# A decoder layer on one core: a PSUM bank of their own for the attention projection's half steps, early merge loads, another form of the last norm

## The chip, the cores and the metric

One core of one Trainium2 chip runs the whole kernel. TensorE (PE) multiplies, VectorE (DVE), ScalarE (ACT) and GpSimd (POOL) do the rest, and SyncE (SP) issues most transfers. The metric is the device time of one execution in microseconds (us).

## The reference, cut to what matters

One step of a hybrid decoder layer for 512 prompt tokens and 8 x 4 sample tokens (544 in all), `D` = 1024, everything in float32:

```
x <- LN1(alpha*x + 1/2 * gate1 * SwiGLU_1(mod1(x)))
x <- LN2(alpha*x + gate2 * MIX(mod2(x)))
x <- LN3(alpha*x + 1/2 * gate3 * SwiGLU_2(mod3(x)))
y_a = rwkv7_time_mix(...)          # 8 heads x 64, delta-rule state
y_b = nsa attention(...)
m = (g_a * (y_a @ w_out_a) + g_b * (y_b @ w_out_b)) @ w_o
layer_norm: ((x - mean) * rsqrt(var + 1e-5)) * g + b
```

The change touches how `y_b @ w_out_b` is fitted in among the recurrence that gives `y_a`, how the sum of the two gated projections (the merge) gets its operands, and LN3, which gives the output `y`.

## The kernel before

Activations lie with features on the 128 partitions and tokens along the free axis, in 8 feature tiles of 128 x 544 (`xT`). A float32 product is made of three fast ones: every operand is split into a high part (`whi`, an ACT cast, L261) and a low part (`wlo`, a DVE subtraction, L179), and TensorE multiplies high by high, high by low and low by high. A product of one 128-column weight tile over 544 tokens is done as two halves of 272 tokens.

The stages follow each other: first FFN, input projections, attention, the RWKV recurrence, the merge of both branches, the output projection `w_o` with LN2, the second FFN, and LN3 (`LayerNormOut`). A scheduler places the instructions of a stage by priorities when the program is built; on the chip each engine runs its own list strictly in order, and semaphores hold an instruction until its data and its buffers are there.

**Recurrence (about 1020 to 1250 us).** `rw_head` makes one of four pairs of heads; up to four are alive, a new one starting some steps after the last. A head has a front (decays, products of 64 x 64 and 128 x 128), a forward substitution that runs on DVE (tiles `t` and `x`), then many narrow products (32 x 32 by L1687, L1695, L1713; 32 x 512 by L1817), prompt steps one after another (L1780 to L1802) and a tail that writes the head's features to `yah` (high and low part). Nearly all its small results go through `sm()`, the pool `smp` of four PSUM banks; wide ones through `mm()`, two pairs of banks.

**The attention projection `wob_steps`** runs inside this stage, at a lower priority than the heads, one half step at a time when a head says that it has only small work: 12 matmuls of 128 x 128 x 272 into one `sm()` bank (L288 on tiles `ybh`), then a DVE operation that multiplies by the gate (`gst`). After two half steps the tile is stored to device memory (`mbd`, by SP, L1978). There are 8 x 2 half steps.

**Merge (L2026 to L2065).** For each of 8 feature tiles: the weight `w_out_a` (256 KB), the gate `gdr` and `mbd` (272 KB each) are loaded by SP, three tiles ahead; 24 matmuls (L2040) make the product from `yah`; DVE multiplies by the gate, adds `mbd` and makes the low part `ul`; ACT makes the high part `uh`. The old `xT` (272 KB) is loaded back as well. For the first two tiles the three quarters of the product that don't need the last head (k = 0..2) are issued ahead. All loads and weight buffers of this stage come from pools that open only when those of the recurrence are closed. Then eight loads of `w_o` (512 KB) follow on the same queue.

**Second FFN start.** Casts of its weights (L261) share ACT with LN2's normalisation of 8 feature tiles (`xT<-xT,pv`, L193). f counts the column blocks of the gate and up weights; f = 0 and 1 are loaded early.

**LN3.** `feature(qt, k)` transposes feature tile k of 128 tokens into PSUM (L710), `bn_stats` (L712) on DVE every four tiles, and `finish(qt)` does statistics, square root, reciprocal, and then for both halves of 512 features: ACT scales and shifts, DVE multiplies by `ln_g`, POOL or DVE adds `ln_b` (L731), SP stores (L732). Tokens 0 to 255 are handled while the last product still runs on the others; tokens 256 to 511 and the sample tokens come at the end.

## Time and profile before

| | us |
|---|---|
| three runs: lowest, median, highest | 1766.15, 1773.29, 1776.47 |
| profiled execution: device time | 1771.6 |
| profiled execution: span | 1769.4 |
| PE busy in the span | 1666.9 (94%) |
| DVE, ACT, POOL busy | 879.5, 603.1, 242.3 |
| mean granted TensorE clock | 0.974 of full |

In a view by windows a row gives a stretch, its length, the busy us of PE, PE's weight loads, DVE, ACT and POOL with instruction counts, then the granted TensorE clock (1.00 is 2.4 GHz, 0.50 is 1.2 GHz), the share of the DMA engines and the GB/s. In a timeline a row is start, length, engine, line, operation, out<-in, shapes, count, and in brackets the idle time ahead with its releaser. The chain that ended last names, back from the end, what each piece of work had waited for. SPq is the queue of SP. Matmul ends are modelled, so lengths of matmuls overlap; the distance of starts is the cost of one.

### The profile page before, as it was taken

The numbers are of one execution on the slowest core, as the hardware profiler recorded it, in microseconds if no ns is written. First come the engines' busy times: TensorE is split into PE (matmuls) and PEld (weight loads), VectorE is DVE, ScalarE is ACT, GpSimd is POOL, SyncE is SP. The second block draws the span as 40 slices with busy tenths as digits, with TensorE's granted clock in tenths as the row PEclk, the third lists the DMA queues.
The fourth block names the chain that finished last, engine by engine and source line by source line (L and its number), as shares of the span: only waits on it lengthen the run. The fifth ranks groups of instructions, "written<-read, shape, count | busy, mean of one in ns | idle before, by whom it ended". The sixth has DMA issues, their size and how long they took to land.

```text
span 1769.4 us, 34773 instructions
## 1 busy us (share of the span) xinstructions
PE 1666.9 (94%) x14710; PEld 1515.0 (86%) x14710; DVE 879.5 (50%) x1834; ACT 603.1 (34%) x1095; POOL 242.3 (14%) x290
## 2 busy tenths in 40 slices
PE   5999999999999899898998999999799999999995
PEld 4888899999999888677786978777788999999994
DVE  6664233223335736555567277675677233233345
ACT  4343221221224543334445333332456221222221
POOL 6640000000000213545300021111011000000001
PEclk9999999999999999999999989997899999999998
DMA  7863662653434285565431431201742232323321
GB/s 275 303 192 114 196 195 87 194 193 113 143 105 99 89 262 160 171 203 159 122 110 49 123 100 32 65 22 34 241 115 89 86 89 85 94 76 96 91 63 51
DMA packets 261788, 224.98 MB, mean 127 GB/s; under 512 B 28880, under 2 KB 225915, under 8 KB 261376
## 3 DMA queue, kind: packets, MB, share of 16 engines
q1 hardware_dynamic: 246008, 182.60, 34.6%
q0 software_dynamic: 9728, 33.56, 5.9%
q10 hardware_dynamic: 5896, 6.60, 1.1%
q8 instruction: 116, 1.90, 0.5%
q14 instruction: 40, 0.33, 0.1%
HBM read 199.55 MB, written 23.17 MB: 126 GB/s over the span
## 4 chain that ended last, share of the span: by engine, by line
PE 79%; DVE 7%; issue 5%; DMA 3%; ACT 3%; POOL 2%; SPq 0%; ACTq 0%; POOLq 0%; DVEq 0%
PE mm L279 45%; PE mm L288 7%; PE mm L400 5%; PE sm L519 2%; PE sm L288 2%; PE sm L1817 1%; PE mm L2040 1%; PE mm L1519 1%; POOL sraw L1217 1%; PE sm L1163 1%; PE sm L1655 1%; DMA raw<-in_phi_w1t_dram 1%; PE sm L1627 1%; PE mm L1125 1%; DVE xT L173 1%
## 5 line engine op out<-in xcount | busy, mean ns | idle before, releaser
L261 ACT CAST whi<-raw 128x1024 fp32r<-128x1024 f32 (+2 forms) x178 | 177.5, 998 | 657.9 <-PE mm L279 591.8
L279 PE MATMUL mm<-uh,whi 128*128 128x272 f32 (+1 forms) x1888 | 397.2, 292 | 2.5 <-ACT qs L193 1.3
L279 PE MATMUL mm<-uh,wlo 128*128 128x272 f32 (+1 forms) x1888 | 392.5, 289 | 0.3 <-DVE wlo L179 0.3
L279 PE MATMUL mm<-ul,whi 128*128 128x272 f32 (+1 forms) x1888 | 391.9, 288 | 0.0
L179 DVE TENSOR_TENSOR wlo<-raw,whi 128x1024 fp32r<-128x1024 f32 (+2 forms) x178 | 207.0, 1163 | 267.8 <-ACT whi L261 266.3
L279 PEld LDWEIGHTS mm<-uh,whi 128*128 128x128 f32 x1888 | 298.0, 189 | 21.8 <-ACT hh L797 9.2
L279 PEld LDWEIGHTS mm<-ul,whi 128*128 128x128 f32 x1888 | 299.8, 189 | 1.0 <-issue 1.0
L279 PEld LDWEIGHTS mm<-uh,wlo 128*128 128x128 f32 x1888 | 297.3, 189 | 1.7 <-DVE sg L173 0.8
L173 DVE TENSOR_TENSOR sg<-mm,sg 128x544 f32<-128x544 f32 (+1 forms) x47 | 32.3, 688 | 164.4 <-PE mm L279 159.4
L676 POOL TENSOR_TENSOR xT<-xT,mr 128x272 f32<-128x272 f32 x24 | 25.0, 1059 | 600.6 <-DVE xT L173 591.1
L400 PE MATMUL mm<-cx,w1h 128*128 128x256 f32 x512 | 99.8, 290 | 3.7 <-ACT cx L352 1.9
L279 PE MATMUL mm<-hh,whi 128*128 128x256 f32 x480 | 99.3, 288 | 0.0
L279 PE MATMUL mm<-hh,wlo 128*128 128x256 f32 x480 | 99.0, 288 | 0.0
L279 PE MATMUL mm<-hlo,whi 128*128 128x256 f32 x480 | 98.9, 287 | 0.0
L400 PEld LDWEIGHTS mm<-cx,w1h 128*128 128x128 f32 x512 | 82.0, 192 | 11.2 <-issue 6.7
L279 PEld LDWEIGHTS mm<-hh,whi 128*128 128x128 f32 x480 | 76.7, 188 | 1.7 <-ACT hh L797 1.7
L279 PEld LDWEIGHTS mm<-hlo,whi 128*128 128x128 f32 x480 | 76.9, 188 | 0.0
L279 PEld LDWEIGHTS mm<-hh,wlo 128*128 128x128 f32 x480 | 76.8, 188 | 0.0
L400 PE MATMUL mm<-cx,w1l 128*128 128x256 f32 x256 | 73.5, 287 | 0.0
L1217 POOL DMA_INDIRECT sraw<-in_cache_kv_sel_dram,idx x64 | 63.9, 998 | 58.1 <-DMA t_new_kv_win_sample_dram<-sraw 22.6
L182 DVE SCALAR_TENSOR_TENSOR xT<-mm,modT,xT 128x512 f32<-128x512 f32 (+2 forms) x80 | 46.3, 581 | 37.0 <-PE mm L288 37.0
L738 DVE TENSOR_TENSOR rtmp<-mm,modT 128x32 f32<-128x32 f32 x32 | 6.1, 192 | 117.0 <-PE mm L279 117.0
(529 smaller groups left out, 2959.9 us busy)
## 6 DMA issues: line engine op xcount, KB each, us to landing
araw<-in_w_ada_dram SPq DMA_DIRECT2D x56, 512.0 KB
raw<-in_ffn_w_gate_dram SPq DMA_DIRECT2D x44, 512.0 KB
raw<-in_ffn_w_up_dram SPq DMA_DIRECT2D x44, 512.0 KB
raw<-in_w_in_dram SPq DMA_DIRECT2D x36, 512.0 KB
raw<-in_ffn_w_down_dram SPq DMA_DIRECT2D x32, 448.0 KB
raw<-in_w_ada_dram SPq DMA_DIRECT2D x16, 512.0 KB
raw<-in_ffn_w_down_dram SPq DMA_DIRECT2D x16, 512.0 KB
sraw<-in_state_kv_win_dram SPq DMA_DIRECT2D x16, 256.0 KB
```

The source lines that it names most:

```text
L173: V.tensor_tensor(out, a, b, ALU.mult)
L179: V.tensor_tensor(out, a, b, ALU.subtract)
L182: V.scalar_tensor_tensor(out, a, s, b, o0, o1)
L261: S.copy(hv, raw)
L279: T.matmul(ps[:m, h, :n], ww[:, k, :m], xx[:, c0:c0 + n], start=(k == 0 and j == 0), stop=(k == nk - 1 and j == 2))
L288: T.matmul(ps[:, :n], ww[:, k, :], xx[:, c0:c0 + n], start=(k == 0 and j == 0), stop=(k == nk - 1 and j == 2))
L400: T.matmul(pss[:, o, 256 * v:256 * v + 256], ww[:, v, o, jj, :], xx, start=(jj == 0 and j == 0), stop=(jj == 7 and j == 2))
L519: T.matmul(hold["ps"][32 * q:32 * q + 32, :], silT[:, k, :], raws_[i][:, h * 512:(h + 1) * 512], start=(k == 0), stop=(k == KT - 1), tile_ ...
L676: G.tensor_tensor(n, n, mr, ALU.subtract)
L1125: T.matmul(ps[:, g, 0:nk], qT[64 * g:64 * g + 64, i, qt * 128:(qt + 1) * 128], kvt[br, 0][64 * g:64 * g + 64, 0:nk], start=True, stop=True)
L1163: T.matmul(acc[64 * g:64 * g + 64, kt * 128:], kvtok[br][:, kt, 128 + 64 * g:192 + 64 * g], pt_[g][:, 512 * kt:384 * kt + 512], start=(br ...
L1217: G.indirect_dma_start(out=t, out_offset=None, in_=seltab, in_offset=bass.IndirectOffsetOnAxis(ap=idx8[:, c * NB + b:c * NB + b + 1], axis=0))
```

## The change

1. PSUM: `smp` (four banks) is closed when the heads are created. The heads' small products then use three banks (`smr`), and the half steps of `wob_steps` one bank of their own (`wb`). After the merge's first parts there are four again (`sm2`).
2. `mbd` is stored by POOL's queue instead of SP's.
3. Merge: the weights of tiles 0 and 1 are loaded and split from the recurrence's own pool, and the parts k = 0..2, then k = 3, are issued before that pool closes. Gates and `mbd` go into the rows of the result tiles `u[0]`, `u[1]` that they end in, four tiles ahead. The load of `xT` tile n is held until tile n is merged, by a POOL copy of one column from `ga`.
4. LN3 of tokens 256 to 543: `late(k)` transposes g·x (scaled by ACT), and keeps running sums of x and x squared; `close()` adds these up over the partitions by matmuls with ones, and corrects the transposed tiles in PSUM by one matmul per bank with rows of -g and b, so that a single scaled copy is left for each bank. The rows are prepared at LN3's construction, near the second FFN's start (memset, four row loads, a cast, a subtraction, two row copies by DMA, two ACT operations on 64 x 1024).

```diff
+    stm = ExitStack()
+    smp = pool("smp", 4, PSUM, stack=stm)
...
             for h in range(2):
                 cs = slice(HT * h, HT * h + HT)
-                ps = sm()
+                ps = wbp.tile([128, 512], F32, tag="wb", name=nm("wb"))
                 dense_half([ps], [w], lambda k: (ybh[0][:, k, :], ybh[1][:, k, :]), 4, HT * h, HT)
...
-            SY.dma_start(mbd[n], g_)
+            G.dma_start(mbd[n], g_)
...
     heads = [rw_head(ht) for ht in range(4)]
+    stm.close()
+    smp = pool("smr", 3, PSUM, stack=stm)
+    wbp = pool("wbp", 1, PSUM, stack=stm)
...
+    def merge_w(n):
+        return load_w(wview(woa, 0, 512, n * 128, (n + 1) * 128))
...
+    parts = [(mm(), merge_w(n)) for n in range(2)]
+    for p in parts:
+        merge_part(*p, 0, 3)
+    for p in parts:
+        merge_part(*p, 3, 4)
     str_.close()
     strp.close()
+    stm.close()
+    smp = pool("sm2", 4, PSUM, stack=stm)
...
     def merge_load(n):
-        raw = load_raw(wview(woa, 0, 512, n * 128, (n + 1) * 128))
-        t = [op.tile([128, TOK], F32, tag=tag, name=f"{tag}{n}", bufs=6) for tag in ("gate", "mb")]
-        SY.dma_start(t[0], gdr[0, n])
-        SY.dma_start(t[1], mbd[n])
-        return raw, t
+        if n < KT:
+            if n > 1:
+                raws[n] = load_raw(wview(woa, 0, 512, n * 128, (n + 1) * 128))
+            SY.dma_start(u[0][:, n, :].bitcast(F32), gdr[0, n])
+            SY.dma_start(u[1][:, n, :].bitcast(F32), mbd[n])
...
-        stt(v272(ga), v272(ga), 1.0, halves(ps), ALU.add, ALU.mult)
-        add(ga, ga, mb)
+        ga = op.tile([128, TOK], F32, tag="ga", name=nm("ga"), bufs=3)
+        stt(v272(ga), v272(u[0][:, n, :].bitcast(F32)), 1.0, halves(ps), ALU.add, ALU.mult)
+        add(ga, ga, u[1][:, n, :].bitcast(F32))
         S.copy(u[0][:, n, :], ga)
         sub(u[1][:, n, :], ga, u[0][:, n, :].bitcast(F32))
+        G.tensor_copy(xT[:, n, 0:1], ga[:, 0:1])
         SY.dma_start(xT[:, n, :], xsp[:, n, :])
...
+        def late(self, k):
+            z = xT[:, k, 256:TOK]
...
+            act(sq, z, AF.Square)
+            act(self.xs[:, k, :], z[:, 256:], AF.Copy, scale=gcol)
+            act(self.xg[k % 3], z[:, 0:256], AF.Copy, scale=gcol)
...
+                for o_, a, b in zip(self.run, self.old, (z, sq)):
+                    add(o_, a, b)
...
+            for j in range(2):
+                T.matmul(self.ps[j][k // 4][:, (k % 4) * 128:(k % 4 + 1) * 128],
+                         self.xg[k % 3][:, 128 * j:128 * j + 128], ident, is_transpose=True, start=(k % 4 == 0), stop=False)
+        def close(self):
...
+            st = mm()
+            for j, tag in enumerate("zq"):
+                hi, lo = [lnp.tile([128, NL], F32R, tag=tag + c_, name=nm("lh")) for c_ in "hl"]
+                S.copy(hi, self.run[j])
+                sub(lo, self.run[j], hi.bitcast(F32))
+                T.matmul(st[:, j, 0:NL], onesr, hi, start=True, stop=False)
+                T.matmul(st[:, j, 0:NL], onesr, lo, start=False, stop=False)
+                T.matmul(st[:, j, 0:NL], onesr.bitcast(F32), self.last[j], start=False, stop=True)
+            A, B, sg, lhs = slice(0, 64), slice(64, 128), self.sg, self.lhs
+            act(sg[B], st[B, 0, 0:NL], AF.Square)
+            S.copy(lhs[A], st[A, 0, 0:NL])
+            sub(sg[B], st[B, 1, 0:NL], sg[B])
+            sub(lhs[32:64], st[32:64, 0, 0:NL], lhs[32:64].bitcast(F32))
+            act(sg[B], sg[B], AF.Sqrt, bias=eps_ln[B])
+            V.tensor_copy(lhs[B], sg[B])
+            sub(lhs[96:128], sg[96:128], lhs[96:128].bitcast(F32))
...
+            for q, dst, m, ps in out:
+                yo = self.wk.tile([128, D], F32, tag="yo", name=nm("yo"), bufs=3)
+                for hf in range(2):
+                    c = slice(512 * hf, 512 * hf + 512)
+                    T.matmul(ps[hf][:m], lhs[:, 128 * q:128 * q + m], self.rows[:, c], start=False, stop=True)
+                    if hf == 0:
+                        act(yo[:m, c], ps[hf][:m], AF.Copy, scale=r[:m, q:q + 1])
+                    else:
+                        ts(yo[:m, c], ps[hf][:m], r[:m, q:q + 1], None, ALU.mult, ALU.bypass)
+                    SY.dma_start(dst[:, c], yo[:m, c])
...
     def final(h, n):
-        for qt in ((0, 1) if h == 0 else (2, 3)):
-            lno.feature(qt, n)
+        if h:
+            lno.late(n)
+        else:
+            for qt in range(2):
+                lno.feature(qt, n)
```

The change also moves instructions, since the scheduler orders anew. Line numbers of the changed kernel are higher: L288, L1627, L1687, L1695, L1817, L2040 and L261 of before are L289, L1711, L1771, L1779, L1901, L2111 and L262 there. Three places follow.

**PE, the first head's substitution and what follows it.** `sig` feeds the products just ahead of it, `t` and `x` are its results, `ybh` is the attention's output. Before, the half step stands behind the first narrow products:

```order
L1572 MATMUL sm_11251<-cst_r,sig_11128 128x64
L1687 MATMUL sm_11257<-t_1523_11206,f_10994 32x32 x32
L1817 MATMUL sm_11295<-wide_11291,tk_11035 64x512
L288 MATMUL sm_11311<-ybh_10555,whi_11307 128x272
L288 MATMUL sm_11311<-ybh_10556,whi_11307 128x272
L288 MATMUL sm_11311<-ybh_10555,wlo_11308 128x272
```

In the changed kernel, at the same place:

```order
L1656 MATMUL sm_11258<-cst_r,sig_11135 128x64
L289 MATMUL wb_12076<-ybh_10555,wlo_12073 128x272
L289 MATMUL wb_12076<-ybh_10555,whi_12072 128x272
L289 MATMUL wb_12076<-ybh_10556,whi_12072 128x272
L289 MATMUL wb_12076<-ybh_10555,wlo_12073 128x272
```

```order
L1771 MATMUL sm_11264<-t_1523_11213,f_11001 32x32 x32
L1901 MATMUL sm_11302<-wide_11298,tk_11042 64x512 x2
L1901 MATMUL sm_11302<-wide_11299,tk_11042 64x512 x2
L1779 MATMUL sm_11339<-x_1522_11211,w_1533_11263 32x32 x32
L1720 MATMUL sm_11382<-cst_g,e_10960 128x128 x4
```

The changed kernel has two half steps (24 matmuls) between the products ahead of the substitution and L1771, and none among the narrow ones; three more half steps (36 matmuls) stand earlier still, among the head's L1711 products. Before, these five and more stood behind the substitution.

**SP, the end of the recurrence and the merge's first loads.** `uh` and `ul` are the rows of `u[0]` and `u[1]`. Before:

```order
L1978 DMA mbd_13825<-gst_13791 128x544
L2063 DMA xT_13838<-xsp 128x544 x2
L2031 DMA gate_13852<-gdr_0_10389 128x544
L250 DMA raw_13850<-in_w_out_a_dram 128x4x128
L2032 DMA mb_13853<-mbd_11410 128x544
L250 DMA raw_13856<-in_w_out_a_dram 128x4x128
```

The changed kernel (`raw` of tiles 0 and 1 stands a dozen and more rows earlier, among the heads' loads):

```order
L1889 DMA out_new_wkv_prompt_dram<-so_13733 64x2x64
L2140 DMA uh_13922<-gdr_0_10389 128x544
L2141 DMA ul_13923<-mbd_11417 128x544
L2140 DMA uh_13922<-gdr_1_10457 128x544
L2141 DMA ul_13923<-mbd_11964 128x544
L251 DMA raw_13928<-in_w_out_a_dram 128x4x128
L2140 DMA uh_13922<-gdr_2_10527 128x544
L2141 DMA ul_13923<-mbd_12146 128x544
L251 DMA raw_13932<-in_w_out_a_dram 128x4x128
```

The stores of `mbd` and the first loads of `xT` are no longer ahead of the merge's loads; the last `raw` shown (tile 3) takes the slot of tile 1's weight and so waits for the last matmul of that tile's first part.

**ACT, the second FFN's start.** Before, the cast of the f = 2 gate weight (the first L261 row) stands ahead of three normalisations:

```order
L193 ACTIVATE sg_14850<-mm_15034 128x272
L261 CAST whi_15144<-raw_15142 128x1024
L797 CAST hh_14851<-sg_14850 128x272
L261 CAST whi_15150<-raw_15148 128x1024
L193 ACTIVATE xT_13838<-xT_13838,pv 128x512 x3
```

In the changed kernel (L717 is the cast of LN3's rows, L881 is L797 of before):

```order
L717 CAST whi_14865<-raw_14864 128x1024
L194 ACTIVATE sg_14878<-mm_15062 128x272
L194 ACTIVATE xT_13912<-xT_13912,pv 128x512 x3
L881 CAST hh_14879<-sg_14878 128x272
L194 ACTIVATE xT_13912<-xT_13912,pv 128x512
L262 CAST whi_15172<-raw_15170 128x1024
```

The f = 2 gate cast has moved behind the rows' cast and four normalisations.

## Rows read from the trace of the kernel before

**Rows 1.** The page: span, busy us of each engine, and one group of instructions.
```profile
span 1769.4 us, 34773 instructions
...
PE 1666.9 (94%) x14710; PEld 1515.0 (86%) x14710; DVE 879.5 (50%) x1834; ACT 603.1 (34%) x1095; POOL 242.3 (14%) x290
...
L179 DVE TENSOR_TENSOR wlo<-raw,whi 128x1024 fp32r<-128x1024 f32 (+2 forms) x178 | 207.0, 1163 | 267.8 <-ACT whi L261 266.3
```

**Rows 2.** Windows: busy us of PE, PEld, DVE, ACT, POOL; granted clock; DMA share; GB/s.
```profile
1040.00:1050.00 10.00, 7.44 (x76) 4.86 (x74) 9.08 (x31) 5.31 (x15) 2.24 (x2) 1.00 0.10 25
1050.00:1060.00 10.00, 9.16 (x82) 6.49 (x83) 7.91 (x11) 0.00 (x0) 2.74 (x2) 0.50 0.23 62
...
1200.00:1210.00 10.00, 10.00 (x64) 5.38 (x63) 4.35 (x9) 1.75 (x3) 1.04 (x1) 0.51 0.19 57
```

**Rows 3.** Chain that ended last, 1230 to 1300 us: start, length, work.
```profile
1251.26 5.61 DMA raw<-in_w_out_a_dram
...
1257.55 7.33 PE mm L2040 x42
...
1265.78 15.32 PE mm L2040 x120
...
1288.45 5.15 DMA raw<-in_w_o_dram
...
1296.49 3.62 PE mm L288 x27
```

**Rows 4.** By tile or line: least, median, largest ns; first and last start.
```profile
L288 PE MATMUL sm<-ybh,wlo x64: 285/290/488, 1056.3 to 1248.4; 128*128 128x272 f32 x64
...
L179 DVE TENSOR_TENSOR yah<-e,yah x1: 726/726/726, 1250.6 to 1250.6; 128x544 fp32r<-128x544 f32 x1
...
L2040 PE MATMUL mm<-yah,wlo x64: 286/289/428, 1258.6 to 1283.8; 128*128 128x272 f32 x64
```

**Rows 5.** Windows of the merges, columns as in rows 2.
```profile
1251.00:1261.70 10.70, 4.15 (x19) 4.15 (x19) 2.09 (x6) 3.67 (x5) 0.00 (x0) 0.52 1.04 332
1261.70:1284.00 22.30, 22.14 (x177) 21.95 (x176) 17.62 (x27) 12.35 (x20) 0.00 (x0) 1.00 1.01 307
```

**Rows 6.** DMA traffic from 1248 to 1300 us.
```profile
DMA packets 19223, 14.85 MB, mean 286 GB/s; under 512 B 699, under 2 KB 16020, under 8 KB 19220
```

**Rows 7.** Timeline of PE, two heads: start, length, work, idle ahead.
```profile
1050.84 3.06 PE L1687 MATMUL sm<-t,f 32*32 32x32 f32 x64 [2.35 <-DVE t L1671]
...
1055.72 0.82 PE L288 MATMUL sm<-ybh,whi 128*128 128x272 f32 x2
...
1058.74 2.62 PE L1817 MATMUL sm<-wide,tk 32*64 32x512 f32 x6
...
1101.14 1.91 PE L1687 MATMUL sm<-t,f 32*32 32x32 f32 x64
```

**Rows 8.** Timeline of ACT, then of PE, at the second FFN's start.
```profile
1364.55 1.04 ACT L261 CAST whi<-raw 128x1024 fp32r<-128x1024 f32 x1
...
1366.76 2.23 ACT L193 ACTIVATE xT<-xT,pv 128x512 f32<-128x512 f32 x3
...
1368.58 0.41 PE L279 MATMUL mm<-uh,whi 128*128 128x272 f32 x2
```

**Rows 9.** The end: one row of the chain, then timelines of DVE, ACT and SP.
```profile
1749.59 1.30 DVE lst L712 x2
...
1753.09 3.03 DVE L173 TENSOR_TENSOR yo<-yo,lno 128x512 f32<-128x512 f32 x3 [0.25 <-ACT yo L193]
...
1761.30 0.68 DVE L731 TENSOR_TENSOR yo<-yo,lno 32x512 f32<-32x512 f32 x1
...
1751.03 0.29 ACT L193 ACTIVATE lrs<-lmv,eps_ln 128x1 f32<-128x1 f32 x1 [21.43 <-DVE lmv L719]
...
1752.28 2.79 ACT L193 ACTIVATE yo<-sm,lrs 128x512 f32<-128x512 f32 x4
...
1762.00 0.33 SPq L732 DMA_DIRECT2D out_y_sample_dram<-yo  x1
```

More of the change, by code (lines that the diff above doesn't have):

```diff
@@ L150, in build @@
     mmp = pool("mmp", 2, PSUM)
-    smp = pool("smp", 4, PSUM)
+    stm = ExitStack()
+    smp = pool("smp", 4, PSUM, stack=stm)
     cnt = {"ev": 0, "n": 0}
@@ L606, in mod_sample @@
         V.tensor_tensor(bt(out), bt(out), modT[:, sh, k, 1:9].unsqueeze(2).to_broadcast([128, NB, NT]), ALU.add)
-    HT = TOK // 2
+    HT, NL = TOK // 2, TOK - 256
     def ln_prep(wk, k, h, run):
@@ L694, in __init__ @@
         def __init__(self, wk, i):
-            self.wk, self.t = wk, {}
+            self.wk, self.t, self.i = wk, {}, i
             self.gb = [wk.tile([128, D], F32, name=f"lno{j}") for j in range(2)]
@@ L699, in __init__ @@
                 SY.dma_start(t, bass.AP(src.tensor, src.offset, [[0, 128], [1, D]]))
+            fx = [yap.tile([128, 4 * TOK], dt, tag=f"yah{j}", name=f"lnx{j}") for j, dt in enumerate((F32R, F32))]
+            self.rows, self.lhs = fx[0][:, 0:D], fx[0][:, D:D + NL]
+            o_ = 0
+            for name, n in (("xg", (256,) * 3), ("run", (NL,) * 2), ("sg", (NL,)), ("xs", (KT * NS,))):
+                setattr(self, name, [fx[1][:, o_ + sum(n[:j]):o_ + sum(n[:j + 1])] for j in range(len(n))])
+                o_ += sum(n)
+            self.sg, self.xs = self.sg[0], self.xs[0].rearrange("p (k t) -> p k t", k=KT)
+            raw = wp.tile([128, wn], F32, tag="raw", name=nm("raw"), bufs=4)
+            hi = wp.tile([128, wn], F32R, tag="whi", name=nm("whi"), bufs=2)
+            rest = wp.tile([128, wn], F32, tag="raw", name=nm("raw"), bufs=4)
+            G.memset(raw, 0.0)
+            for j, name in ((0, "ln_g"), (32, "ln_g"), (64, "ln_b"), (96, "ln_b")):
+                SY.dma_start(raw[j:j + 1, :], I[name][0, i:i + 1])
+            S.copy(hi, raw)
+            sub(rest, raw, hi.bitcast(F32))
+            for a in (0, 64):
+                SY.dma_start(raw[a + 1:a + 2, :], rest[a:a + 1, :])
+            for a, sgn in ((0, -1.0), (64, 1.0)):
+                act(self.rows[a:a + 64], raw[a:a + 64], AF.Copy, scale=sgn)
         def col(self, tag, n):
@@ new lines, in close @@
+        def close(self):
+            pair = mm()
+            for k in range(KT):
+                T.matmul(pair[:NS, k // 4, (k % 4) * 128:(k % 4 + 1) * 128], self.xs[:, k, :], ident, is_transpose=True,
+                         start=(k % 4 == 0), stop=False)
+            st = mm()
[14 more added lines that the diff above has]
+            sub(lhs[96:128], sg[96:128], lhs[96:128].bitcast(F32))
+            r = self.col("lrs", 3)
+            out = [(0, O["y_prompt"][0, 256:384, :], 128, self.ps[0]), (1, O["y_prompt"][0, 384:512, :], 128, self.ps[1]),
+                   (2, O["y_sample"].rearrange("b t d -> (b t) d"), NS, (pair[:, 0], pair[:, 1]))]
+            for q, _, m, _ in out:
+                T.transpose(st[:m, 1, 288 + 64 * q:352 + 64 * q], sg[B, 128 * q:128 * q + m], ident[B, B])
+                V.reciprocal(r[:m, q:q + 1], st[:m, 1, 288 + 64 * q:289 + 64 * q])
+            for q, dst, m, ps in out:
[8 more added lines that the diff above has]
+                    SY.dma_start(dst[:, c], yo[:m, c])
@@ L1994, in build @@
     yap = pool("yap")
-    yah = [yap.tile([128, 4, TOK], F32R, name=f"yah{i}") for i in range(2)]
+    yah = [yap.tile([128, 4, TOK], F32R, tag=f"yah{i}", name=f"yah{i}") for i in range(2)]
     str_ = ExitStack()
@@ L2013, in build, with merge_part @@
         pass
+    def merge_w(n):
+        return load_w(wview(woa, 0, 512, n * 128, (n + 1) * 128))
+    def merge_part(ps, w, k0, k1):
+        hv, lv = w
+        for k in range(k0, k1):
+            for j, (ww, xx) in enumerate(((hv, yah[0]), (hv, yah[1]), (lv, yah[0]))):
+                for h in range(2):
+                    T.matmul(ps[:, h, 0:272], ww[:, k, :], xx[:, k, 272 * h:272 * h + 272],
+                             start=(k == 0 and j == 0), stop=(k == 3 and j == 2))
+    parts = [(mm(), merge_w(n)) for n in range(2)]
[3 more added lines that the diff above has]
+        merge_part(*p, 3, 4)
     str_.close()
     strp.close()
+    stm.close()
+    smp = pool("sm2", 4, PSUM, stack=stm)
     wp, wn = pool("wp2"), 1024
@@ L2101, in final @@
     def final(h, n):
-        for qt in ((0, 1) if h == 0 else (2, 3)):
-            lno.feature(qt, n)
+        if h:
+            lno.late(n)
+        else:
+            for qt in range(2):
+                lno.feature(qt, n)
     ffn(1, u, 8, wk, [lambda k=k: ln_affine(1, k) for k in range(KT)], early, mid, down_slots, None, lnp, final)
-    for k in range(KT):
-        lno.feature(4, k)
+    lno.close()
     stx.close()
+    stm.close()
     es.close()
```

31 lines of the change are left out of this document (14 added, 17 removed).

## The prediction, made before the changed kernel ran

> **What bounds the kernel now.** I read the page first: PE is busy for 1666.9 of 1769.4 us [rows 1], so only about 100 us without matmuls and the stretches at the lower clock are on offer. Then I looked at windows for the places where PE stands or is slow. In the recurrence PE is idle for 2.6 us of the ten from 1040 and 0.8 us of the next ten, and its clock is at 0.50, the 1.2 GHz level, from 1050 to 1060 and at 0.51 from 1200 to 1210 [rows 2]. Next the chain of waits at the merge: the first merge matmul waits for a w_out_a load of 5.61 us [rows 3]. The last half step starts its last matmul at 1248.4 and ends it some 0.3 us later [rows 4], the first merge matmul starts at 1257.55 [rows 3]: 8.9 us without a matmul, after which the clock has fallen (0.52 in 1251 to 1261.7) [rows 5]. Last, the end: the last statistics start at 1749.59, behind the last transposes, and the last store is issued at 1762.0 [rows 9].
>
> **Merge and w_o loads.** Call T the moment at which the last head's features are ready: 1250.6 + 0.73 = 1251.4 [rows 4]. The last merge matmul starts at 1283.8 [rows 4], so the merges end at 1284.1, T + 32.7. One matmul costs 15.32/120 = 0.128 us [rows 3], a tile's 24 cost 3.06. In the changed kernel tiles 0 and 1 have their weights during the recurrence, and their parts k = 0..2 (36 matmuls, 4.6 us) fit under the last head's tail, where PE now stands. After T remain 12 matmuls (1.5 us) and six tiles (18.4 us): T + 19.9, a gain of 12.8 us if loads keep up. They may not. From 1248 to 1300 the queue moved 14.85 MB at 286 GB/s [rows 6], with the DMA share above 1.0 in both windows [rows 5], and PE still waited for w_o at 1288.45 [rows 3]. The bytes stay. What can move ahead of T are three gates, three mbd and three pieces of w_out_a, 6 x 0.279 + 3 x 0.262 = 2.5 MB or 8.6 us at that rate; but the load of tile 3's weight waits on SP for the last matmul of tile 1 (T + 1.5), and everything behind it, so up to 4.5 us of that lead is lost again (from the tail's start, about T - 3). So if loads decide, the gain is 4 to 8.6 us, if PE decides 12.8. I take 8.5, nearer the loads, since the waits that end last there are DMA's. What is late next is w_o: its first pieces are now behind the held xT loads. The Trainium skill ("DMA: Bandwidth & Descriptors", section "Where 436 GB/s comes from") puts the HBM side of one core at about 358 GB/s; by that page the 12.4 MB left would take 34.6 us, and an estimate of the gain would be the full 12.8 us, with a sum 4.3 us lower. The two windows show 332 and 307 GB/s [rows 5], under it.
>
> The gate and mbd loads straight into u, and the store of mbd on POOL's queue, take SP's issue slots out of the way; DVE's and ACT's operations for a tile stay as they are. I cost them at nothing: POOL is busy for 242.3 us in all [rows 1]. The eight one-column POOL copies only hold back xT, which nobody needs before the output projection.
>
> **The half steps in the recurrence.** A half step costs 12 matmuls. At 1055.72 one starts, and the next narrow product follows at 1058.74 [rows 7]: 3.0 us at the lower clock, where 12 x 0.128 = 1.5 us would do at the higher. The narrow products suffer too: 64 of L1687 took 3.06 us at 1050.84, after 2.35 us of waiting for DVE's substitution, and 1.91 us at 1101.14 [rows 7]. In the changed kernel 24 of these matmuls stand in the place where PE waits for the substitution: they take 3.1 us, of which 2.5 were idle (10 - 7.44) [rows 2]. That is a gain of 2.5. The first block no longer runs at the lower clock: 1.5 more. The same holds for a block in the slow window at 1200 [rows 2], which is now done earlier: 1.5. Together 5.5. Against it: 36 matmuls now stand ahead of the substitution and delay it by up to 4.6 us, but they are no longer behind it, so this is a move, not a cost, as long as PE is the limit there (9.16 and 10.00 of 10 us busy) [rows 2].
>
> Three banks instead of four for the heads: the trace has no such wait. The lower bound is nothing, as PE has no idle time at all in 1200 to 1210 [rows 2], and until now a half step took one of the four banks anyway. For an upper bound take one wait of an eviction's length, 0.70 us (2.79/4) [rows 9], for each of the 16 half steps that used to share: 11 us. I take 1.5, near the row without idle time. The clock of the narrow stretch, now without any dense block in it, is open by 3.06 - 1.91 = 1.15 us per 64 small products [rows 7]; with five or six such groups in the heads that wait, plus or minus 6. The recurrence together: -5.5 + 1.5 = -4, between -12 and +13.
>
> **The second FFN's start.** ACT is the neighbour that waits here. Before, the cast of the f = 2 gate starts at 1364.55 and PE's first matmul with it at 1368.58 [rows 8]. Now LN3's rows (1.05, as any 128 x 1024 cast) and four normalisations (2.23 for three, 0.74 for one) [rows 8] stand ahead of it, with a short cast of 0.4: it starts at 1368.9 and ends at 1370.0, and the low part follows on DVE, 1.16 us on the average [rows 1]. PE wants the first at 1368.58 and the second 0.25 us later: a stall of 1.4 to 2.6 us. I take +2.2. What hid it, ACT's lead of four microseconds, is gone; the next weights are needed 6 us later and are in time.
>
> **The last norm.** Transposes, squares, running sums and scalings for the second half now run under the last product: ACT was idle for 21.43 us until 1751.03 [rows 9]. What is left at the end: one square and one pair of matmuls for the last tile, then square, subtraction, root, two casts with their subtractions in a chain, a matmul, and three evictions on each of ACT and DVE. A 512-column operation takes 0.68 on DVE and 0.70 on ACT [rows 9]; these have 288 columns, so I take 0.45 for each of eight steps (3.6), 0.4 for each of three visits to PE (1.2, by the 0.41 of two matmuls in [rows 8]), and three evictions (2.1 to 2.3): about 7.1 us from 1749.3, so 1756.4 against 1762.0 [rows 9]. Before, 1.30 us of bn_stats, 3.03 us for three multiplications and all the rest were in that row [rows 9]. Gain 5.6; with 0.7 a step 3.6, with 0.3 a step 6.8. The 7.4 us from the last issue to the end of the span stay.
>
> **The sum.** -8.5 - 4.0 + 2.2 - 5.6 = -15.9 us against the profiled execution's 1771.6: 1755.7. The median of the runs is 1.7 us above that execution, so I forecast 1757.
>
> **Rivals.** A: *three banks are too few.* PE then stands before a head's product until ACT or DVE has read an older one, as it stands for DVE at 1050.84, and the clock stays low more often. If each ten microseconds from 1050 to 1240 had the 2.56 idle us of the first window, 19 x 2.56 = 49 us would be lost; from 0.85 us in each (16 us) it eats all the gains, and with half of the 49, 24.5, plus the clock's 6, the time is 1773.3 - 15.9 + 30.5 = 1788, slower. For it: the heads' products are many and short. Against: PE's windows are full now, with a half step often holding one of the four. The Trainium skill ("TensorE: Matmul & The Clock Gate", section "A second HAM failure mode: psum-queue depth-cycling") speaks against the change in the same way: it tells of a kernel whose PE, cycling through PSUM banks, paused so often and briefly between groups that its clock kept falling and rising. The drop at 1050, after a window with 2.6 us of pauses, agrees with that; that fewer banks bring such pauses, no row shows.
>
> B: *the loads give the merge's gain back, and the recurrence keeps its time.* Then -4 - 0 + 2.2 - 5.6 = -7.4, and 1766: within 0.5%. For it: a DMA share above 1.0 for 50 us. That the early loads don't come early, since SP's queue holds them behind a wait, is the same case.
>
> C: *the clock gains more.* With half steps ahead of the narrow stretch PE doesn't pause, and both slow windows of [rows 2] run at the higher level: 4 to 5 us each instead of 1.5, and PE-bound merges (12.8). Then -12.8 - 10 + 2.2 - 5.6 = -26 and 1747.
>
> **How the numbers follow.** The forecast has 0.50, C 0.26, B 0.16, A 0.08. The measurement of this kernel can tell about 0.5% (8.9 us) from no change, so faster means under 1764.4: the forecast and C, 0.76; the same is B, 0.16; slower is A, 0.08. The range leaves out A and the far ends of C and B: from 1745, C with a little to spare, to 1770, where B loses 4 us more in the banks.
>
> **What would show it.** Right: the first merge matmul follows the last half step without a gap, merges end about 24 us after T, the clock stays at its higher level there; the window that holds the first head's substitution has under 0.5 us of idle PE; a stall of some 2 us on an ACT cast before f = 2; the last store issued some 7 us after the last product's matmul. Wrong: PE waiting for ACT f or DVE reads in the recurrence's windows (A), waits for DMA of w_out_a or w_o that sum to over 5 us (B), or a clock at 0.5 through the heads' narrow products for longer than now.

## The result, and the profile after

The change makes the kernel slower: 1786.55 us in the median (1783.62 to 1789.55) against 1766.77 (1763.10 to 1776.47) for the kernel before in the same comparison, a ratio of 1.0098 with an interval of 1.0071 to 1.0125. (The ratios in this text are those on record; they are not the quotients of the medians, here 1.0112.) The forecast was 1757 with a range of 1745 to 1770. The profiled execution of the changed kernel took 1786.33 us. This is its page: span, busy time of the engines, and two groups of instructions (line, operation, count; busy us and mean ns).

```profile
span 1784.6 us, 34888 instructions
...
PE 1702.6 (95%) x14727; PEld 1536.4 (86%) x14727; DVE 877.1 (49%) x1835; ACT 612.8 (34%) x1121; POOL 247.9 (14%) x304
...
L280 PE MATMUL mm<-uh,whi 128*128 128x272 f32 (+1 forms) x1888 | 397.5, 292 | 3.3 <-ACT qs L194 1.3
...
L180 DVE TENSOR_TENSOR wlo<-raw,whi 128x1024 fp32r<-128x1024 f32 (+2 forms) x178 | 206.1, 1158 | 262.3 <-ACT whi L262 260.7
```

Against [rows 1] the span is 15.2 us longer, and PE is *busy* for 35.7 us more, with 17 matmuls more. That is the first hint: PE did not wait longer, its matmuls took longer.

To see where, I laid both traces beside each other at five moments: T, the end of the last head's low part (as in the prediction); the end of the last merge matmul (L2111 here, L2040 before); the start of LN2's first reciprocal (`rstd`); the start of the last residual (a DVE operation on `xT`); the end of the span. All in us.

| | T | T to last merge matmul | T to LN2's reciprocal | from there to the last residual | from there to the end |
|---|---|---|---|---|---|
| before | 1251.4 | 32.7 | 64.4 | 432.9 | 20.8 |
| after | 1274.3 | 25.7 | 60.9 | 436.5 | 12.9 |
| difference | +22.9 | -7.1 | -3.5 | +3.6 | -7.9 |

(Differences are taken before rounding.) Those of columns 1, 3, 4 and 5 add up to 15.1, the span's 15.2 but for rounding. Everything that the change was to bring after T is there, in part; what it loses is 22.9 us before T, nearly all inside the recurrence (the first product of a head, which opens it, starts 1.6 us later than before).

Windows of the recurrence in the changed kernel (columns as in [rows 2]):

```profile
1040.00:1050.00 10.00, 10.00 (x36) 5.84 (x35) 2.54 (x6) 0.00 (x0) 0.00 (x0) 0.58 0.24 67
1050.00:1060.00 10.00, 10.00 (x79) 7.89 (x77) 7.63 (x30) 4.25 (x6) 0.00 (x0) 0.91 0.01 2
...
1200.00:1210.00 10.00, 9.99 (x161) 8.37 (x157) 7.62 (x24) 1.55 (x3) 0.00 (x0) 0.90 0.03 12
1210.00:1220.00 10.00, 10.00 (x42) 6.86 (x42) 2.75 (x9) 0.56 (x1) 0.00 (x0) 0.66 0.01 2
```

The reader is to look at the counts, not at the busy time. From 1040 to 1050 PE is busy for all ten microseconds, and has done 36 matmuls in them; before it did 76 in 7.44 us [rows 2]. The slow window at 1050 is gone, as the prediction said, but there is one at 1040 now (0.58: mostly at the 1.2 GHz level), and one at 1210 (0.66).

The timeline of PE in the first of these stretches tells what stands there:

```profile
1038.78 0.39 PE L289 MATMUL wb<-ybh,whi 128*128 128x272 f32 x1
1039.10 0.43 PE L1711 MATMUL sm<-ar,e 64*64 64x128 f32 x2
1039.46 0.39 PE L289 MATMUL wb<-ybh,wlo 128*128 128x272 f32 x1
1039.78 0.43 PE L1711 MATMUL sm<-ar,e 64*64 64x128 f32 x2
1040.13 0.39 PE L289 MATMUL wb<-ybh,whi 128*128 128x272 f32 x1
...
1045.01 0.59 PE L289 MATMUL wb<-ybh,whi 128*128 128x272 f32 x1
1045.53 0.69 PE L1711 MATMUL sm<-ar,e 64*64 64x128 f32 x2
1046.15 0.59 PE L289 MATMUL wb<-ybh,whi 128*128 128x272 f32 x1
```

Single matmuls of a half step (`wb`, 128x128 of the array) take turns with single products of a head (`sm`, L1711, which use a quarter of the array, 64x64, and are recorded as two matmuls each). The starts of two half-step matmuls are 0.68 us apart (1039.46 - 1038.78), later 1.14 (1046.15 - 1045.01), where the clock is at its lower level. There is no idle time in brackets: no wait is recorded. In the kernel before the same products (L1627 there) stand in one piece, 32 records in 1.59 us, and the half steps stand in blocks of twelve.

### The profile page after: what moved, and what is told of

It reads as the page before. It is cut to its first block, busy times and chain, and to the rows that moved or that the text cites. A ratio compares the mean times of both kernels' runs of the same rounds, so it can differ in the third digit from the quotient of the medians.

```text
span 1784.6 us, 34888 instructions
## 1 busy us (share of the span) xinstructions
PE 1702.6 (95%) x14727; PEld 1536.4 (86%) x14727; DVE 877.1 (49%) x1835; ACT 612.8 (34%) x1121; POOL 247.9 (14%) x304
## 4 chain that ended last, share of the span: by engine, by line
PE 79%; DVE 6%; issue 6%; ACT 3%; POOL 3%; DMA 2%; SPq 0%; POOLq 0%; ACTq 0%; DVEq 0%
PE mm L280 46%; PE mm L289 6%; PE mm L401 5%; PE sm L520 2%; PE wb L289 2%; POOL sraw L1301 1%; PE sm L1711 1%; PE sm L1901 1%; PE sm L1739 1%; PE mm L1603 1%; PE sm L1247 1%; PE mm L2111 1%; DMA raw<-in_phi_w1t_dram 1%; DMA raw<-in_w_o_dram 1%; PE mm L1209 1%
## 5 line engine op out<-in xcount | busy, mean ns | idle before, releaser
L262 ACT CAST whi<-raw 128x1024 fp32r<-128x1024 f32 (+2 forms) x178 | 177.3, 997 | 645.1 <-PE mm L280 593.9
L677 POOL TENSOR_TENSOR xT<-xT,mr 128x272 f32<-128x272 f32 x24 | 25.1, 1062 | 530.8 <-DVE xT L174 518.6
```

The source lines that it names most:

```text
L262: S.copy(hv, raw)
L677: G.tensor_tensor(n, n, mr, ALU.subtract)
```

## The experiments

**Is it the interleaving? (e1, e2)** The changed kernel, with the twelve matmuls of a half step held together by a high priority for all but the first. Nothing else is changed in the program: three banks for the heads, one for the half steps. (The scheduler shifts some of the heads' instructions with them: of PE's other matmuls from 990 us to T, 3030 of 3157 keep their order.)

```diff
-                dense_half([ps], [w], lambda k: (ybh[0][:, k, :], ybh[1][:, k, :]), 4, HT * h, HT)
+                for q in range(0, 12, 12):
+                    for i, (k, j, ww, xx) in enumerate(mms[q:q + 12]):
...
+                        if i == 0:
+                            one()
+                        else:
+                            with tc.high_priority(offset=6000):
+                                one()
```

> The changed kernel with one difference: the 12 matmuls of a half step stay together (all but the first get a higher priority), still in their own bank, with three banks for the heads. The matmuls of the half steps then stand in 17 runs on PE instead of 67 (15 in the kernel before). Theory 1, each break of a small-tile sequence by a 128x128 matmul and back costs PE about 0.4 us: 50 breaks fewer give back 50 x 0.4 = 20 us, the last head's features (T) come at about 1253 instead of 1274 and the time is 1764 to 1768. Theory 2, three banks are too few for the heads: T stays at 1270 or later and the time at 1782 to 1788. Theory 3, the early place of the half steps, ahead of the first head's substitution, delays it: some 5 us come back at most, 1780.

Measured: 1756.34 us, a ratio to before of 0.9934 (0.9907 to 0.9961); T at 1243.0, so 31.3 us before that of the changed kernel and 8.4 before that of the kernel before. That is more than theory 1 expected (T at 1253, 1764 us at the least); theories 2 and 3 fall. Here is the same place in e1's timeline of PE, and two of its windows:

```profile
1039.02 0.29 PE L2063 MATMUL wb<-ybh,wlo 128*128 128x272 f32 x1
1039.14 0.41 PE L2063 MATMUL wb<-ybh,whi 128*128 128x272 f32 x2
1039.39 0.29 PE L2063 MATMUL wb<-ybh,wlo 128*128 128x272 f32 x1
1039.61 1.59 PE L1711 MATMUL sm<-ar,e 64*64 64x128 f32 x32
1041.13 1.16 PE L1739 MATMUL sm<-dd,cst_t 128*128 128x128 f32 x8
```

```profile
1040.00:1050.00 10.00, 10.00 (x103) 8.40 (x100) 8.83 (x34) 4.25 (x6) 0.00 (x0) 1.00 0.30 84
1050.00:1060.00 10.00, 9.74 (x133) 7.78 (x133) 9.63 (x26) 4.73 (x13) 3.81 (x4) 1.00 0.18 54
```

All 32 records of L1711 take 1.59 us again, the ten microseconds from 1040 hold 103 matmuls and not 36, and the clock is full in both windows.

e2 holds three together and not twelve.

> The changed kernel, with the matmuls of a half step kept together in threes: 40 runs on PE instead of 67. Theory 1 (breaks cost 0.4 us each): 27 breaks fewer give back about 11 us, 1775, between the changed kernel and the groups of 12. Theory 2 (three banks): no change, 1782 to 1788. Theory 3 (place): no change.

Measured: 1771.3 us, ratio 1.0005 (0.9979 to 1.0031): between the two, as an interleaving with up to four pieces for each half step should be. The pieces can be counted in the list of PE, as runs of half-step matmuls with nothing between: 67 in the changed kernel, 17 in e1, 40 in e2, 15 in the kernel before. Against e1 the changed kernel has 50 more and T is 31.3 us later: 0.63 us for each. e2 has 23 more and its median is 15.0 us longer: 0.65 for each.

That is not what a piece costs by itself. e2's profiled execution is its shortest, 1757.52 us (one of the ten took 1762.34, the other eight 1770.6 to 1772.9). With the same 40 pieces its T is 1246.4, only 3.4 us after e1's. What sets it apart from the eight is the granted clock: 0.982 over the span, 0.973 to 0.976 in them. The clock is also a large part of what sets the changed kernel apart from e1. From 1030 to 1250, in the kernel before, the changed kernel and e1:

```profile
1030.00:1250.00 220.00, 211.10 (x3008) 166.70 (x3003) 151.70 (x409) 70.81 (x139) 32.46 (x40) 0.88 0.18 46
...
1030.00:1250.00 220.00, 218.64 (x2723) 168.51 (x2724) 134.90 (x375) 65.96 (x131) 37.85 (x48) 0.82 0.18 47
...
1030.00:1250.00 220.00, 211.80 (x3094) 170.34 (x3093) 162.45 (x428) 76.79 (x150) 39.33 (x52) 0.93 0.26 71
```

A mean of 0.82 between the levels 1.00 and 0.50 is 79 us of the 220 at the lower one; 0.88 is 53 us, 0.93 is 31. If all work took twice as long there, 24 of the 31 us between the changed kernel and e1 would be the clock's, and 13 of the 22.9 against the kernel before. The clocks of the whole spans (0.970 and 0.980 of some 1770 us) give 18 between the changed kernel and e1. These are estimates; by them the changes of tile size alone cost 7 to 13 us of the 31. The lower clock comes with the interleaving in all executions of these two, 0.969 to 0.972 in the changed kernel's six and 0.979 to 0.982 in e1's eight, and in eight of ten of e2. Why it does was not tried.

**Is it the split of the banks? (e3, e4)** e3 is the changed kernel with one pool of four banks for heads and half steps together, as before.

```diff
-                ps = wbp.tile([128, 512], F32, tag="wb", name=nm("wb"))
+                ps = sm()
...
-    smp = pool("smr", 3, PSUM, stack=stm)
-    wbp = pool("wbp", 1, PSUM, stack=stm)
+    smp = pool("smr", 4, PSUM, stack=stm)
```

> The changed kernel with its first part undone: heads and half steps share four banks again; merge, store queue and last norm as changed. 15 runs of half-step matmuls on PE. Theories 1 and 2 both give back the recurrence: T at 1251 to 1254. The rest of the change is then seen alone: by the trace of the changed kernel merges -7.1, w_o loads +3.5, second FFN's start +2.0, second FFN's middle +1.7, end -7.9, together -7.8 against the kernel before: about 1759 where that has 1766.8.

e4 is the kernel before with the split of the banks alone.

```diff
-                ps = sm()
+                ps = wbp.tile([128, 512], F32, tag="wb", name=nm("wb"))
...
+    smp = pool("smr", 3, PSUM, stack=stm)
+    wbp = pool("wbp", 1, PSUM, stack=stm)
```

> The kernel before with only the first part of the change: three banks for the heads and one for the half steps. Half-step matmuls in 65 runs on PE. Theories 1 and 2: the recurrence is 20 us longer and the time 1785 to 1789 (1.010 to 1.013 of the kernel before). If the loss of the changed kernel came from the store on POOL's queue or the early merge weights among the heads' loads instead, it stays within 3 us of the kernel before.

Measured: e3 1765.51, ratio 0.9969 (0.9939 to 1.0000), T at 1256.2, 15 runs of half-step matmuls. e4 1796.74, ratio 1.0152 (1.0106 to 1.0199), T at 1275.2, 65 runs. Both miss their expectations on the long side: e3 was to take about 1759 us, e4 at most 1.013 of the kernel before. The split alone does the whole harm: T is where the changed kernel has it (1274.3). The rest of the change is worth little, 1.0152 - 1.0098 or half a per cent by this pair (whose intervals overlap), 0.3 by e3 (whose interval reaches 1). And e1 beside the changed kernel shows that it isn't the *number* of banks: with three for the heads e1 has an earlier T than any kernel with four. With a bank of their own the half steps come in 65 pieces, where they must share in 15. Presumably the scheduler, which then finds their matmuls ready at any time, puts one wherever it sees a gap; why it sees one between two heads' products was not tried.

**What does one turn cost, and is it the size of the array's tile? (e12)** The kernel before, with matmuls added at its end, all in one pair of banks, waiting for nothing (of the edit, the calls alone):

```diff
+    bench("B", 100)
+    bench("S", 24)
+    bench("B", 48)
+    bench("BS", 24)
+    bench("B", 96)
+    bench("F", 24)
+    bench("B", 48)
+    bench("BF", 24)
+    bench("B", 48)
```

B is one 128x128 matmul of 272 columns, S two float32 products on two 64x64 tiles, F one 128x128 float32 product of 128 columns. "BS" puts the two in turn.

> The kernel before, with matmuls into one unused pair of PSUM banks added at its end, whose results nobody reads: 24 pairs of 64x64 tiles alone (64x128, float32), then the same pairs in turn with one 128x128 matmul of 272 columns each, then 24 128x128 matmuls of 128 columns in float32 alone, and these in turn with the 272-column ones; blocks of the latter (48 to 100) stand between. The time is longer by this work and says nothing. Theory D (PE loses time where the array's tile size changes): at the full clock the 64x64 pairs alone go at about 0.1 us a pair and the 272-column matmuls at 0.126, the turns of big and small at 0.65 to 0.7, not 0.23; the turns of two kinds that both use 128x128 at the sum of the two. Rival O (any change of operands or of the operation costs the time): both kinds of turns are longer than their sum by about 0.45 us. Rival B (the loss came from the change of PSUM banks or from waits on buffers): neither is, since all stand in one bank and wait for nothing.

```profile
1765.05 5.46 PE L2121 MATMUL mm<-xT 64*64 64x128 f32 x96
1770.43 6.40 PE L2117 MATMUL mm<-w 128*128 128x272 f32 x49
1776.77 0.43 PE L2121 MATMUL mm<-xT 64*64 64x128 f32 x4
1777.13 0.39 PE L2117 MATMUL mm<-w 128*128 128x272 f32 x1
1777.45 0.44 PE L2121 MATMUL mm<-xT 64*64 64x128 f32 x4
...
1792.93 12.30 PE L2117 MATMUL mm<-w 128*128 128x272 f32 x96
1805.07 5.52 PE L2124 MATMUL mm<-xT 128*128 128x128 f32 x48
1810.34 6.39 PE L2117 MATMUL mm<-w 128*128 128x272 f32 x49
1816.57 0.38 PE L2124 MATMUL mm<-xT 128*128 128x128 f32 x2
1816.71 0.37 PE L2117 MATMUL mm<-w 128*128 128x272 f32 x1
1816.92 0.38 PE L2124 MATMUL mm<-xT 128*128 128x128 f32 x2
```

By distances of starts: B alone (1805.07 - 1792.93)/96 = 0.126 us, S alone (1770.43 - 1765.05)/24 = 0.224, F alone (1810.34 - 1805.07)/24 = 0.220. A turn of B and S takes 1777.45 - 1776.77 = 0.68, which is 0.33 more than 0.126 + 0.224. A turn of B and F takes 1816.92 - 1816.57 = 0.35, the sum of the two. So here operands, operation and records change at no cost; a change between 128x128 and 64x64 of the array costs. The rivals O and B fall. The size that I had expected was off: S alone takes 0.22, not 0.1. The turn itself came out as expected, and it is the same 0.68 as in the changed kernel, where only half as much (two records, 0.11 us) stands between two half-step matmuls; there the loss is 0.68 - 0.126 - 0.11 = 0.44 us for each. The Trainium skill ("TensorEngine Tiling (Array Packing)", section "Key Properties") says that a change of the tiling mode drains TensorE. It gives no time; the trace agrees that such a change costs, and puts 0.33 to 0.44 us on leaving the mode and coming back, at the full clock. Not every piece is such an excursion, as some stand beside other 128x128 products: from 1000 us to T PE changes between 128x128 and smaller tiles 184 times in the changed kernel and 108 times in e1. These are 38 excursions more, 13 to 17 us at that price; that is at or above what the clock leaves of the 31.

**What are the other edits worth? (e5 to e8)** Each is e1 with one of the others undone. They ran on another chip, whose runs of the kernel before have a median of 1776.3, so only ratios compare with e1's 0.9934 (0.9907 to 0.9961). e5 has the old last norm:

> The kernel with groups of 12 (e1, 1756.3 us), with the last norm of before on all tokens and without its rows. From the traces of before and of the changed kernel the new norm gives 7.9 us at the end (last residual to the end of the span 20.8 against 12.9), and costs 2.0 at the second FFN's start and 1.7 before its end: without it 1760.5. If the sum of the prediction's own terms held (-5.6 and +2.2): 1759.7. If the new norm is worth nothing, 1756.

Measured: 1764.05, ratio 0.9936 (0.9915 to 0.9957). From the last residual to the end it takes 21.3 us, e1 12.8. e6 has the old merge, with the store of `mbd` still on POOL's queue:

> e1 with the merge of before: loads only after the recurrence's pools close, gates and mbd into tiles of their own, no hold on xT. The traces say that the new merge gives 7.1 us up to the last merge matmul and loses 3.5 to later w_o loads: without it 1760. If the loads decide it all and the new merge is worth nothing, 1756; if PE decided, as much as 12.8 more, 1769.

Measured: 1759.39, ratio 0.9909 (0.9877 to 0.9941), and 25.2 us from T to the last merge matmul, no more than with the new merge. e7 prepares LN3's rows at the last product's first half instead of the second FFN's start:

> e1 with the norm's rows prepared when the last product's first half starts, not at the second FFN's start; ACT's order there is that of before. The stall ahead of f = 2 (0.77 + 0.49 us in e1's trace) goes: 1754 to 1755. If ACT is full there anyway, no change.

Measured: 1762.21, ratio 0.9931 (0.9908 to 0.9955). The stall at the second FFN's start is gone, but the last product's first half now waits. PE's waits there, in e7, from 1690 to 1705 (engine and tile, what was waited for, us in total, times, longest):

```profile
PE sm L735 <- DVE xT L183: 1.2, 2, 0.6
PE mm L289 <- ACT uh L262: 0.6, 1, 0.6
PE mm L289 <- DVE w L180: 0.6, 1, 0.6
PE mm L289 <- DVE ul L180: 0.6, 1, 0.6
```

These alone are 3.0 us where e1's PE waits 0.35 us in that half, for the 1.3 saved. e8 drops the POOL copies that hold the `xT` loads back:

> e1 without the POOL copies that hold each xT load until its tile is merged. If xT's loads then run ahead of the merge's, the merges end some 2 to 3 us later and w_o comes earlier: between 1755 and 1758. If the hold is what delays w_o (3.5 us), 1753.

Measured: 1760.3, ratio 0.9911 (0.9877 to 0.9944). From T to LN2's reciprocal it takes 57.0 us; e5 and e7, with the hold and on the same chip, take 56.6 and 56.4, so the hold is not seen to cost anything there. The intervals of all four overlap e1's: none of these edits has an effect that the times resolve, and only the stretches of the traces say something.

**Where does the merge's gain come from? (e9 to e11)** e6 raised the question, since it has the old merge and is as quick. These three ran on one chip. e9 is e1's kernel again:

> The same kernel as e1 (the change, with the twelve matmuls of a half step kept together), run again as the base for the two that follow on the same chip. Expected by all theories: 6 to 16 us faster than before (ratio 0.991 to 0.9965), and 24 to 26 us from the last head's features to the last merge matmul. If from there to LN2's first statistics it is 56 us instead of e1's 60.8, the shorter time in the four runs e5 to e8 came with their chip and not from their edits.

e10 is e1 with the merge as in the kernel before and `mbd` stored by SP again (so what is left of the change is the split of the banks, with blocks, and the last norm); of the edit, the store alone:

```diff
-            G.dma_start(mbd[n], g_)
+            SY.dma_start(mbd[n], g_)
```

> e1's kernel with the merge as it was in the kernel before (loads three tiles ahead from pools opened after the recurrence, no held xT loads) and with mbd stored by SyncE again. Theory S (the store on GpSimd's queue is what shortens the merge: on SyncE's queue it stands, with its wait, ahead of the merge's first loads): 32 to 34 us from the last features to the last merge matmul, some 7 to 8 us more than e11, and a time 5 to 8 us above e11's. Theory W (the early weights and the loads straight into u shorten the merge): also 32 to 34 us, but then e11 is as long as this one.

e11 is e6's kernel again:

> The same kernel as e6: e1's with the old merge, but with mbd's store on GpSimd's queue. Theory S: 24 to 26 us from the last features to the last merge matmul, as in e9, and a time within 3 us of e9's. Theory W: 32 to 34 us, as in e10, and some 7 us above e9; e6's 25.2 would then have been its chip's.

| | us | ratio, interval | last half step's last matmul | T | T to last merge matmul | T to LN2's reciprocal |
|---|---|---|---|---|---|---|
| before | 1767.15 | | 1248.4 | 1251.4 | 32.7 | 64.4 |
| e9 | 1757.62 | 0.9947 (0.9925 to 0.9969) | 1229.7 | 1242.2 | 25.8 | 58.9 |
| e10 | 1753.09 | 0.9904 (0.9865 to 0.9942) | 1237.6 | 1251.2 | 24.7 | 55.0 |
| e11 | 1757.32 | 0.9944 (0.9921 to 0.9967) | 1233.1 | 1249.5 | 25.6 | 56.0 |

(The stretches of before are those of its one profiled execution.) Both theories fall: with old merge *and* SP's store e10 needs 24.7 us, not the 32 to 34 that either expected. e9's 58.9 us to the reciprocal lie between the 56 and the 60.8 that its expectation set apart: with this merge the stretch takes 56.4 to 60.9 us from one trace to the next (e7 and the changed kernel), and what the chips have to do with it stays open. What differs from the kernel before is when the half steps are done. The chain that ended last, in e10:

```profile
1236.16 1.77 PE wb L2063 x12
...
1237.96 2.80 DMA xT<-xsp
...
1240.85 0.81 ACT xT L194
1241.68 0.81 ACT xT L194
...
1248.41 8.33 PE mm L2143 x42
```

Behind the last half step at 1236.16 the loads start at once, 13 us ahead of T (1251.2). Before, the last half step ended some 0.3 us after 1248.4, its store was issued at 1249.32, and only then did the queue come to `xT` (L2063) and to the `w_out_a` load of [rows 3]:

```profile
1248.94 0.36 DVE gst L182
1249.32 0.32 SPq L1978
...
1249.69 0.42 SPq L2063
```

So the new merge is one of two ways to the same end. It helps where the half steps end late (25.7 us in the changed kernel and 25.1 in e3 against 33.4 in e4 and 32.7 before, whose merge is the old one); where they end early (e6, e10 and e11 beside e1 and e9) there is nothing left to gain. In e10 ACT works on the early `xT` (1240.85) ahead of the last head's own operations, and T is 9 us later than in e9; but 7.9 of these are there at the last half step (1237.6 against 1229.7), before ACT starts on it, so it can have cost some 1 us. The order of the recurrence is nearly the same in both; the granted clock from 1000 us to T is 0.90 in e10 and 0.94 in e9. The times of e9, e10 and e11 don't differ by more than their intervals allow. e10 has the lowest ratio of all kernels run, though those of e6 and e8 are within 0.001 of it; all kernels with blocks (e1, e5 to e11) lie below the kernel before by their whole interval.

## Why the prediction was wrong, point by point

**The step that failed** is "so this is a move, not a cost", in the part on the half steps. It took the 24 matmuls that fill the wait as 24 times 0.128 us, and the 36 ahead of them likewise: as a block, as [rows 7] show one. The order gave them as single matmuls between single 64x64 products, and I priced them without asking what a matmul costs between two of another tile size. [Rows 7] show nothing of the kind, since before a half step stands in one piece. At 1038 twelve of them, with 20 records of L1711 between, took 9.7 us (1038.09 to 1047.81) instead of 1.5 and 1.0. With it fell the two terms for the clock, 1.5 us each for blocks that would no longer run at the lower level: from 1030 to 1250 the granted clock went from 0.88 to 0.82, by the estimate above a loss of up to 13 us, and only "plus or minus 6" had been allowed for it. So the sign turned: -4 was forecast for the recurrence, +21.3 measured (22.9 less the 1.6 that it starts later).

**The idea under it was right.** With blocks (e1) the half steps fill the wait, the clock stays full at 1050, and T is 8.4 us earlier (10.6 counted from the recurrence's start), within the -12 to +13 that I gave and beyond the -4 that I took. It is one execution: e9 has T at 1242.2, but e5 and e7, with the same recurrence on another chip, at 1251.9 and 1248.8.

**Rival A had nearly the right time and not the right cause.** It said 1788 and got 1786.6, but by three banks that make PE wait, and from a median before of 1773.3 that six runs put at 1766.77: its loss was 15 us and not 20. PE's busy time in the windows above is 10.00 of 10, where waits would show as idle time (from 1030 to 1250 it idles for 1.4 us, before for 8.9), and e1 keeps the three banks and gains. So it is no confirmation of A. Its test, PE waiting for reads by ACT or DVE in the recurrence's windows, is not what the trace shows; the other, the clock at the lower level for longer, is there, and is a consequence: it is full in e1's windows at 1040 and 1050, and e1's program differs in how these matmuls are kept together alone. The section of the Trainium skill that I set beside A ("TensorE: Matmul & The Clock Gate", "A second HAM failure mode: psum-queue depth-cycling") speaks of pauses between groups; here the clock fell at 1042 in a stretch without a recorded pause.

**Merge and `w_o`:** -8.5 was the term; the merge itself gave -7.1, and 3.6 of that went back before LN2, so -3.5 is left. What took it back is what the text named as late next, `w_o`. The chain in the changed kernel, near the last merge matmul:

```profile
1297.58 6.81 DMA raw<-in_w_o_dram
...
1306.83 6.18 DMA raw<-in_w_o_dram
```

Two waits for transfers stand there, where [rows 3] have one of 5.15. I named it and gave it no price. That the held `xT` loads are what delays it is not shown: without the hold (e8) the stretch is no shorter than with it on the same chip. The store on POOL's queue was costed at nothing; e10 beside e11 agrees for kernels whose half steps end early.

**Second FFN's start:** +2.2 forecast, +1.8 measured: counted from LN2's reciprocal, f = 2's first matmul comes 0.9 us later than before, and the matmuls behind the second stall 1.8 later. PE's timeline has the two stalls that the text described, on the cast and on the low part; as idle time they sum to 1.24 us:

```profile
1388.92 0.53 PE L280 MATMUL mm<-uh,whi 128*128 128x272 f32 x2 [0.76 <-ACT whi L262]
...
1390.18 0.52 PE L280 MATMUL mm<-uh,wlo 128*128 128x272 f32 x2 [0.48 <-DVE wlo L180]
```

**Last norm:** -5.6 forecast, -7.9 measured from the last residual to the end. Of that, 1.8 us (3.6 less 1.8) went back between the second FFN's start and the residual; with the old norm (e5) the stretch from the reciprocal to the residual is 434.5 us where e1 has 437.7. The term is mis-sized in two places that go opposite ways. SP's last rows, [rows 9] before and here after:

```profile
1778.74 1.97 SPq L798 DMA_DIRECT2D out_y_prompt_dram<-yo  x4
1780.80 1.20 SPq L798 DMA_DIRECT2D out_y_sample_dram<-yo  x2
```

The last store is issued at about 1781.7 (two issues in 1.20 us, the second 0.33 long), 10.0 us after the last residual's start at 1771.72, against 13.4 before (1762.00 - 1748.64): only 3.4 gained. But the span ends 2.9 us later, where I had said that "the 7.4 us from the last issue to the end of the span stay". With the old norm (e5) that tail is 8.1 us (1764.3 - 1756.21), so it belongs to the old norm. What it consists of was not tried.

**The sum.** Had the half steps come in blocks, the number 1757 would have held, but in part by luck: e1's kernel took 1756.34 and 1757.62 (e9) on two chips where the kernel before had medians of 1766.47 and 1767.15, a gain of 9.5 to 10.1 us where 15.9 were forecast from a median of 1773.3. The range left out A and with it every case in which the recurrence loses more than a few microseconds. Its bound for the recurrence (+13) was for waits; for the cost of the interleaving, which the order showed in advance, there was no term at all. Three slips did not decide: the recurrence's own terms give +11.5 at the most and not +13; [rows 5] show the DMA share above 1.0 for 33 us, not 50; and the low part of f = 2's weight is wanted 0.50 us after the high part, not 0.25 (before, PE's `uh,wlo` starts at 1369.08).

## What to carry to other kernels

When matmuls on the whole array and products on parts of it share PE, keep each kind in runs. In the turns measured here an excursion from one tile size to the other and back cost 0.33 to 0.44 us at the full clock, with two or four records in it. The profile books this as busy time, so count matmuls per window beside the busy share. And look at the granted clock of the whole stretch: here its fall cost at least as much as the excursions themselves. A buffer that two streams share can be what keeps them in blocks; giving one a buffer of its own can free the scheduler to interleave them, so read the new order for how finely it does so before pricing the move. And before moving loads forward, ask what they wait for: here doing the small work in front of them earlier gave as much as rewriting the stage.

## What the runs showed of the hardware that I had not expected

- A turn between the two tile sizes lasted 0.68 us at the full clock with two records of 64x64 between (changed kernel) and with four (e12): the two more cost nothing. At the lower clock, with two, it was 1.14 us.
- A change of operands, weights and number format at the same tile size cost nothing: 0.35 us a turn for 0.126 + 0.220 in e12.
- In e12 turns went on for 16 us (1776.77 to 1792.93) and stayed at 0.68 to 0.69 us each, so at the full clock; in the changed kernel they slowed down after 4 us (1038.09 to 1042.12). e12 had twice as many small records in a turn and a dense block ahead. Which of these matters stays open.
- One and the same kernel has runs that differ by more than 10 us, and the granted clock goes with them: e2 had 1757.52 us at 0.982 and 1770.64 at 0.974; 0.008 of 1757 us is 14.
